# Two experts of a routed feed-forward layer: whole-array matmuls in three passes on weights split in high and low parts

## The chip, the cores and the metric

One core of one Trainium2 chip runs the whole program. The metric is the device time of one execution, in microseconds (us); lower is better. In the kernel's names, PE is TensorE, DVE is VectorE, ACT is ScalarE and SP is SyncE, whose queue issues the DMAs.

## The reference

Two trunk layers work on 256 latent tokens and 256 context tokens of width 1024: a gMLP mixer and a dense SwiGLU, then a bidirectional recurrent mixer and a layer of eight SwiGLU experts of which each latent token uses two. Only the expert layer is touched. With `h` of 256 x 1024 and expert width 3584:

```
logits = h @ w_router                                  # 256 x 8
top_val, top_idx = top_k(logits, 2);  probs = softmax(top_val)
combine[t, e] = probs of expert e for token t, or 0
for e in range(8):
    out += combine[:, e:e+1] * ((silu(h @ w_gate[e]) * (h @ w_up[e])) @ w_down[e])
```

All arrays are float32. An expert works only on the tokens routed to it; each expert's three weight matrices are 44 MB, and all eight are read from memory once.

## The kernel before

**Ranks and units.** Expert 0 is rank 0 whatever its load, because its weights are fetched before the routing is known. The other seven are ranked by their number of tokens, rank 1 the fullest; SP reads the ranked order from registers, so the addresses of the weights are chosen on the chip (`wsrc`, line 406). A one-hot matmul gathers the tokens of an expert into up to 128 columns (`gather`, line 1230). `units` (line 1173) decides from the counts how a rank runs: with up to 32 tokens its matmuls use 32 columns of the array, four of them side by side (n = 4); with up to 64 they use 64, two side by side (n = 2); with more they use all 128 (n = 1). Ranks 0 to 3 can have an overflow unit for tokens beyond the base unit: a count of 65 to 96 gives a base of 64 and the rest as overflow, a count above 128 a base of 128 and the rest as overflow. The choice is a branch on registers: `tc.If` in `region` (line 1339). Rank 1 takes n = 2 or n = 1, ranks 2 and 3 one of all three.

**Chunks.** The expert width is cut in seven chunks of 512. A chunk needs six slots of weights of 1 MB each (128 x 2048): two of gate, two of down, two of up. `chunk` (line 1289) does them in that order: transposes of the hidden values of an earlier chunk, the gate projection (`proj`, line 1272, matmuls on line 1276), the down projection of the earlier chunk (line 1303), the up projection. Gate and up are 8 matmuls of 512 columns each, down is 8 too. The trace has two records for each float32 matmul. For n > 1 `total` (line 1279) adds the side-by-side partial sums on ACT and DVE. After the base unit the overflow unit, if there is one, runs the same six slots again (`over`, line 1319, tile `xu`).

**Two lanes.** `moe_regions` (line 161) writes the order out by hand. One lane is the ranks 1, 2, 3, the other 0, 7, 6, 5, 4; their chunks are interleaved in proportion to their bytes. `R` is a chunk, `F` a last down projection, `O` and `G` the gathers, `S` the weighted scatter at an expert's end. The down projection lags its gate and up by one chunk in the first lane, two in the second. Two chunks of ranks 1 or 2 never follow each other directly.

**Slots.** `Stream` (line 192) owns a ring of SBUF slots of 1 MB. In the expert stage there are 16: four of `rawp`, one of `raw2`, six of `hlp`, two of `hl2` and three of `raw3` (`RAW3`, line 158). SP issues the loads in the order in which the regions use them; a load waits until its slot has been read by its last reader. For ranks 0 to 3 that is the overflow unit or, without one, the end of the branch on line 1364.

**Three passes.** The dense layers already split their operands. `prep_to` (line 239) casts a weight slot to `float32r` on ACT (`wh`) and subtracts on DVE (`wl`); `mm3` (line 505) then does three matmuls instead of one float32 matmul: high x high, high x low, low x high. A `float32r` matmul is one record.

Of the kernel before, what the change touches and what calls it, by code (L numbers as in the profile page):

```python
# [9 lines left out]
F32 = mybir.dt.float32  # L10
F32R = mybir.dt.float32r
# [143 lines left out]

TM = (1, 1, 1, 0)
WC = (2, 2, 14)
RAW3 = ("wx", "wy", "wz")


def moe_regions():
# [25 lines left out]


LAG = {r: 1 if r in (1, 2, 3) else 2 for r in range(NE)}


class Stream:
# [34 lines left out]
        self.slots += slots  # L227
        self.load()

    def take_raw(self, n):  # L230
        got = [self.raw.pop(self.prep_i + k) for k in range(n)]
        self.prep_i += n
        return got

    def free(self, got):
        self.slots += [s for s, _ in got]
# [32 lines left out]
def block_kernel(ctx, tc, xin, pos, cst, rows, wsT, adaS, adaT, wA, lruG, wr, wM, out):  # L269
# [136 lines left out]
    def wsrc(r, k):  # L406
        if r == 0:
            return wM[k]
        return lambda: wM[bass.ds(base42[r] + k, 1)].rearrange("o p c -> (o p) c")

    for kind, r, c in regs:
        if kind in "RF":
            for w in ("g", "d", "u"):
                cc = c - LAG[r] if w == "d" else c
                if 0 <= cc < NCH:
                    items += [(wsrc(r, 6 * cc + 2 * "gud".index(w) + i), "own") for i in range(2)]
    st = Stream(nc, items, 2)
    st.add_h(hlp, 3)
    st.nh = 0

# [84 lines left out]
    def mm3(o, lh, ll, rh, rl, start, stop):  # L505
        PE.matmul(o, lh, rh, start=start, stop=False)  # L506
        PE.matmul(o, lh, rl, start=False, stop=False)  # L507
        PE.matmul(o, ll, rh, start=False, stop=stop)  # L508
# [620 lines left out]
        ACT.preload_act_table_set("sqrt_and_others")  # L1129
    c_y(0)  # L1130
    c_y(1)
    st.moe([(hlp, f"w{x}{i}") for i in range(3) for x in "hl"] + [(hl2, "wh0"), (hl2, "wl0")])
    hx = hTp.tile([P, 4, D], F32, tag="hTlo", name="hx")
    h2, hg, tg = hx[:, 0:2], hx[:, 2].rearrange("p (n c) -> p n c", n=2), hx[:, 3].rearrange("p (n c) -> p n c", n=2)
    lb = [bank(), bank()]
# [37 lines left out]
    def units(q):  # L1173
        few, m64, cb_, co_ = q[:, 6:10], q[:, 10], q[:, 11], q[:, 12]
        cf = q[:, 4]
        DVE.tensor_scalar(m64, cf, 64.0, 64.0, op0=ALU.is_gt, op1=ALU.mult)
        DVE.scalar_tensor_tensor(m64, cf, 96.0, m64, op0=ALU.is_le, op1=ALU.mult)
        if q is Qr:
            DVE.memset(m64[:, 4:NE], 0.0)
        DVE.tensor_scalar(co_, cf, -128.0, None, op0=ALU.add)  # L1180
        DVE.tensor_add(co_, co_, m64)
        DVE.tensor_scalar(co_, co_, 0.0, None, op0=ALU.max)
        DVE.tensor_sub(cb_, cf, co_)
        for n, (v, lim, m) in enumerate(((cb_, 64, 64), (cb_, 32, 32), (co_, 32, 64), (co_, 32, 32))):
            DVE.tensor_scalar(few[:, n], v, float(lim), -float(m), op0=ALU.is_le, op1=ALU.mult)

    units(Q)
    dup = mp.tile([P, 2, P], F32, name="dup")
# [41 lines left out]
    def gather(x, G, k0, b):  # L1230
        for kk in range(4):
            for t in range(2):
                PE.matmul(b[:, kk * P:(kk + 1) * P], h2[:, t, (k0 + kk) * P:(k0 + kk + 1) * P], G[:, t], start=(t == 0), stop=(t == 1))  # L1233
        xq = x[:, k0:k0 + 4].rearrange("p k s -> p (k s)")
        if k0:
            DVE.tensor_copy(xq, b)
        else:
            ACT.copy(xq, b)

    def gather_parts(E):  # L1240
        G = m2.tile([P, 2, P], F32, tag=f"G{E.s}", bufs=1, name="G")
        sl_ = m2.tile([P, P], F32, tag="sl", bufs=1, name="sl")
        x = m2.tile([P, 8, P], F32, tag=f"x{E.s}", bufs=1, name="x")
        GT = m2.tile([P, 256], F32, tag=f"GT{E.s}", name="GT")
        ps = m2.tile([P, 1], F32, tag=f"ps{E.s}", name="ps")
        E.base = Unit(x, None, tg[:, E.s], GT, ps)

        def last():
            weigh(E, G, GT, ps, nb[0]())
            E.rv = nc.values_load(cnti[0:1, 0, E.e:E.e + 1], engines=ENG, min_val=0, max_val=128)  # L1250
            if E.e < 4:
                E.ro = nc.values_load(cnti[0:1, 1, E.e:E.e + 1], engines=ENG, min_val=0, max_val=128)
            if E.e in (1, 2, 3):
                E.rl = nc.values_load(cnti[0:1, 3, E.e:E.e + 1], engines=ENG, min_val=0, max_val=1)
        return [lambda: onehot(E, G, sl_, 0), lambda: gather(x, G, 0, nb[0]()), lambda: gather(x, G, 4, nb[0]()), last]

# [32 lines left out]
    def chunk(U, n, bt, bg, bu, yb_, raws, first, last, hd, hw, hook=None):  # L1289
        rg, rd, ru = raws  # L1290
        m = P // n
        if rd:
            for kk in range(4):
                PE.transpose(bt[:, kk * m:(kk + 1) * m], hd[0:m, kk * P:(kk + 1) * P], ident[0:m, 0:m])  # L1294
            ACT.copy(U.th[:, 0:4 * m], bt[:, 0:4 * m])  # L1295
        if rg:
            proj(bg, U.x, rg, n)
            ACT.activation(hw[0:m], total(bg, n), AF.Silu)
        if rd:
            for kk in range(4):  # L1300
                r, g = divmod(kk, n)
                for hf in range(2):
                    PE.matmul(yb_[hf][m * g:m * g + m], U.th[:, kk * m:(kk + 1) * m], rd[hf][1][:, kk * 512:(kk + 1) * 512],  # L1303
                              start=(first and r == 0), stop=(last and r == 4 // n - 1), **tp(n, g))
        if rd and hook is not None:
            hook()
        if ru:
            proj(bu, U.x, ru, n)
            DVE.tensor_mul(hw[0:m], hw[0:m], total(bu, n))  # L1309

    def scatter(GT, src):
# [27 lines left out]
    def region(E, c, raws):  # L1339
        p0, p1 = bks[2 * par[0]:2 * par[0] + 2]  # L1340
        lag = LAG[E.e]
        a = (p1, p0, p1, E.base.y, raws, c == lag, c == NCH + lag - 1, *hsel(E, c, E.hh))

        def few_():
            if E.e == 1:
                return chunk(E.base, 2, *a)
# [5 lines left out]
        if E.e in (1, 2, 3):  # L1352
# [61 lines left out]
    pp = ctx.enter_context(tc.tile_pool(name="pp", bufs=1, space=bass.MemoryType.PSUM))  # L1414
    *bks, y0, y1, y2, y3 = [pp.tile([P, 512], F32, tag=f"b{i}", name="ps") for i in range(8)]
    Ys = [mw.tile([P, D], F32, name=f"Y{n}") for n in range(2)]
    Gu = mw.tile([P, 2, P], F32, name="Gu")
    slu = mw.tile([P, P], F32, name="slu")
    ta_ = mw.tile([P, 512], F32, name="ta_")
# [20 lines left out]
    def yrot(E):  # L1440
# [2 lines left out]
            return E.base.y[cyc[0] % 2]  # L1443
        return f
    parts = {}
    for kind, e, c in regs:
        if kind == "O":
            exps[e] = Expert(e, Qr)
            parts[e] = gather_parts(exps[e])
            parts[e][0]()  # L1450
        elif kind == "G":
            for f in parts[e][1:]:
                f()
            start(exps[e])
        elif kind == "S":
            E = exps[e]
            nb[0] = yrot(E)
            scatter(E.base.GT, Ys[E.s])
            if e < 4:
                with tc.If(E.ro > 0):  # L1460
                    DVE.tensor_scalar(E.over.y, E.over.y, E.over.ps, None, op0=ALU.mult)  # L1461
                    scatter(E.over.GT, E.over.y)
            nb[0] = rot
        else:
            E = exps[e]
            par[0] ^= 1
            rg = st.take_raw(2) if c < NCH else None
            rd = st.take_raw(2) if c >= LAG[e] else None
            ru = st.take_raw(2) if c < NCH else None
            region(E, c, (rg, rd, ru))  # L1470
# [44 lines left out]
```

## Time and profile before

| | us |
|---|---|
| three runs | 1848.4, 1852.88, 1853.86 |
| median | 1852.88 |
| the profiled execution | 1844.61 |
| its span | 1842.8 |

The profile is of one further execution, 1.8 us longer than its span and 8.3 us below the median of the runs. The expert stage begins at about 850 us and ends at about 1830 us of the span. A name such as L1276 is a line of the code; a tile such as `raw` is a weight slot. In a table of windows the number after a time is a count of instructions, PEclk is the granted TensorE clock as a share of full speed, and the DMA share is that of the 16 DMA engines together.

### The profile page before, as it was taken

How to read it: one execution, taken by the hardware profiler on the slowest of the kernel's cores; microseconds unless marked ns; L12 is line 12 of the kernel's file. 1: busy time of each engine (PE TensorE's matmuls, PEld its weight loads, DVE VectorE, ACT ScalarE, POOL GpSimd, SP SyncE). 2: the span in 40 equal slices, each digit the busy share in tenths (PEclk: the TensorE clock that was granted, in tenths of full speed). 3: DMA queues.
4: the chain of work that ended last, by engine and by line, in shares of the span. 5: the costliest groups of instructions: out<-in, count | busy, mean ns of one | idle time of the engine just before them, and what ended most of it. 6: DMA issues, size and time to landing. Idle time of an engine off the chain costs nothing. (4 is left out here: it accounts for less than half of the span.)

```text
span 1842.8 us, 21730 instructions
## 1 busy us (share of the span) xinstructions
PE 1667.9 (91%) x8192; PEld 1026.5 (56%) x8192; DVE 835.5 (45%) x1342; ACT 573.8 (31%) x840; POOL 19.4 (1%) x22
## 2 busy tenths in 40 slices
PE   5999999999999999985878789989987999889987
PEld 2888888988888888764434233343333353333332
DVE  3777745569875348985322222333110112132234
ACT  5624224732222247972221121211120112122221
POOL 0000001000000000001000000000000000000000
PEclk9999999999999999997989999999998999999999
DMA  8554424247765313265896778987899899979990
GB/s 362 207 182 160 160 92 155 92 160 254 262 260 206 116 67 115 92 256 234 324 415 281 319 301 340 404 358 295 363 418 418 365 395 360 387 323 387 401 389 24
DMA packets 70421, 492.97 MB, mean 268 GB/s; under 512 B 7968, under 2 KB 8160, under 8 KB 11872
## 3 DMA queue, kind: packets, MB, share of 16 engines
q1 hardware_dynamic: 70240, 490.45, 67.5%
q8 instruction: 127, 2.08, 0.5%
q14 instruction: 54, 0.44, 0.1%
HBM read 489.34 MB, written 1.08 MB: 266 GB/s over the span
## 5 line engine op out<-in xcount | busy, mean ns | idle before, releaser
L1276 PE MATMUL ps<-raw,x 128*64 128x512 f32 (+2 forms) x1792 | 439.9, 610 | 28.0 <-issue 24.9
L1276 PEld LDWEIGHTS ps<-raw,x 128*64 128x64 f32 (+2 forms) x1792 | 163.1, 143 | 260.2 <-issue 247.4
L1303 PE MATMUL ps<-raw,hx 128*32 128x512 f32 (+2 forms) x1120 | 256.5, 616 | 19.3 <-ACT hx L1295 15.1
L522 PE MATMUL ps<-hThi,wh 128*128 128x512 f32 (+1 forms) x736 | 254.4, 347 | 3.0 <-ACT hThi L373 3.0
L523 PE MATMUL ps<-hTlo,wh 128*128 128x512 f32 (+1 forms) x736 | 251.7, 343 | 1.4 <-DVE hTlo L374 1.3
L524 PE MATMUL ps<-hThi,wl 128*128 128x512 f32 (+1 forms) x736 | 252.4, 343 | 0.0
L1283 DVE TENSOR_TENSOR ta__6629<-ps,ta__6629 64x512 f32<-64x512 f32 x112 | 76.5, 683 | 348.8 <-ACT ta__6629 L1282 348.8
L249 ACT CAST wh<-raw 128x2048 fp32r<-128x2048 f32 x69 | 131.6, 1910 | 227.5 <-PE ps L523 114.1
L250 DVE TENSOR_TENSOR wl<-raw,wh 128x2048 fp32r<-128x2048 f32 x69 | 158.8, 2304 | 63.7 <-ACT wh L249 63.0
L1303 PEld LDWEIGHTS ps<-raw,hx 128*32 128x32 f32 (+2 forms) x1120 | 92.1, 137 | 160.5 <-issue 125.2
L388 DVE SCALAR_TENSOR_TENSOR dj<-raw,srow 128x1024 bf16<-128x1024 f32 x128 | 156.2, 1220 | 36.2 <-DMA raw<-in_adaT_dram 32.6
L1282 ACT COPY ta__6629<-ps 64x512 f32<-64x512 f32 x112 | 65.2, 582 | 301.1 <-PE ps L1276 291.1
L522 PEld LDWEIGHTS ps<-hThi,wh 128*128 128x128 f32 x736 | 138.0, 188 | 21.3 <-ACT hThi L373 3.7
L523 PEld LDWEIGHTS ps<-hTlo,wh 128*128 128x128 f32 x736 | 138.1, 188 | 20.8 <-DVE hTlo L374 2.0
L524 PEld LDWEIGHTS ps<-hThi,wl 128*128 128x128 f32 x736 | 138.1, 188 | 18.3 <-issue 0.5
L1309 DVE TENSOR_TENSOR hx<-hx,ps 128x512 f32<-128x512 f32 x14 | 9.6, 688 | 254.9 <-PE ps L1276 179.3
L506 PE MATMUL ps<-wh,ph 128*128 128x512 f32 x304 | 119.4, 393 | 0.0
L508 PE MATMUL ps<-wh,pl 128*128 128x512 f32 x304 | 118.5, 390 | 0.6 <-DVE pl L753 0.5
L507 PE MATMUL ps<-wl,ph 128*128 128x512 f32 x304 | 118.3, 389 | 0.0
L1295 ACT COPY hx<-ps 128x128 f32<-128x128 f32 (+2 forms) x70 | 25.3, 362 | 224.6 <-PE ps L1294 222.8
L1276 PE MATMUL ps<-raw,xu 128*32 128x512 f32 x448 | 69.7, 635 | 21.7 <-DVE accy L1331 11.5
L1286 DVE TENSOR_TENSOR ta__6629<-ps,ta__6629 32x512 f32<-32x512 f32 x70 | 47.5, 678 | 38.0 <-ACT ps L1285 34.2
(327 smaller groups left out, 1672.5 us busy)
## 6 DMA issues: line engine op xcount, KB each, us to landing
raw<-in_wM_dram SPq DMA_DIRECT2D x336, 1024.0 KB, 13.6
raw<-in_wA_dram SPq DMA_DIRECT2D x69, 1024.0 KB, 4.9
raw<-in_adaT_dram SPq DMA_DIRECT2D x40, 1024.0 KB, 4.9
va<-in_adaS_dram SPq DMA_DIRECT2D x4, 1024.0 KB, 11.2
ysum<-in_xin_dram SPq DMA_DIRECT2D x4, 512.0 KB, 5.5
vb<-in_adaS_dram SPq DMA_DIRECT2D x2, 1024.0 KB, 11.9
srow<-in_adaS_dram SPq DMA_DIRECT2D x2, 1024.0 KB, 13.2
lw<-in_lruG_dram SPq DMA_DIRECT2D x8, 256.0 KB, 3.3
```

Source lines behind the costliest of these rows:

```text
L249: self.nc.scalar.copy(wh, raw)
L250: self.nc.vector.tensor_tensor(out=wl, in0=raw, in1=wh.bitcast(F32), op=ALU.subtract)
L388: DVE.scalar_tensor_tensor(j, raw[:, kk * D:(kk + 1) * D], 1.0, srow[:, vv], op0=ALU.mult, op1=ALU.mult, accum_out=adaC[l, bb // 8][:, bb ...
L506: PE.matmul(o, lh, rh, start=start, stop=False)
L507: PE.matmul(o, lh, rl, start=False, stop=False)
L508: PE.matmul(o, ll, rh, start=False, stop=stop)
L522: PE.matmul(o, wh[:, r], hThi[:, kk, c0:c1], start=(kk == 0), stop=False)
L523: PE.matmul(o, wh[:, r], hTlo[:, kk, c0:c1], start=False, stop=False)
L524: PE.matmul(o, wl[:, r], hThi[:, kk, c0:c1], start=False, stop=(kk == 7))
L1276: PE.matmul(o[m * g:m * g + m], x[:, kb, 0:m], raws[kb // 4][1][:, (kb % 4) * 512:(kb % 4 + 1) * 512], start=(r == 0), stop=(r == 8 // n - ...
L1283: DVE.tensor_tensor(out=ta_[0:64], in0=o[0:64], in1=ta_[0:64], op=ALU.add)
L1303: PE.matmul(yb_[hf][m * g:m * g + m], U.th[:, kk * m:(kk + 1) * m], rd[hf][1][:, kk * 512:(kk + 1) * 512], start=(first and r == 0), stop= ...
```

## The change

Ranks 1 and 2 lose their branches. Their base unit always takes up to 128 tokens, and every matmul with a weight is done by `mm3` in `float32r`. The gathered tokens are split in `xh` and `xl`, the transposed hidden values in the two tiles `thl`. The weights are split in pieces of a quarter slot (128 x 512): a cast on ACT, a subtraction on DVE. The split pieces live in a ring of four pairs (`wp`); piece n + 4 is made after the three matmuls of piece n are issued, and four pieces of a chunk's first slot are made ahead, before the region that comes before the chunk. In the order of the loads that first slot moves ahead of the up slots of that earlier region. The ring takes the place of two raw slots (`hl2`), and one slot of `raw3` is dropped, so that 13 of 16 slots are left. Rank 3 and the second lane run as before, and so does the overflow of ranks 1 and 2 beyond 128 tokens.

```
-RAW3 = ("wx", "wy", "wz")
+RAW3 = ("wx", "wy")
+THREE = (1, 2)
...
+def moe_slots(regs):
+    runs = [o for o in regs if o[0] in "RF"]
+    lists = [region_slots(o) for o in runs]
+    for a, b, x, y in zip(runs, runs[1:], lists, lists[1:]):
+        if a[1] not in THREE and b[1] in THREE:
+            n = sum(k[2] != "u" for k in x)
+            x.insert(n, y.pop(0))
+    return [k for x in lists for k in x]
...
-    st.moe([(hlp, f"w{x}{i}") for i in range(3) for x in "hl"] + [(hl2, "wh0"), (hl2, "wl0")])
+    st.moe([(hlp, f"w{x}{i}") for i in range(3) for x in "hl"])
+    wp = [hl2.tile([P, 4, 512], F32R, tag=f"w{x}0", name=f"w{x}p") for x in "hl"]
...
         if q is Qr:
+            DVE.memset(m64[:, 1:3], 0.0)
             DVE.memset(m64[:, 4:NE], 0.0)
...
+        if q is Qr:
+            DVE.memset(few[:, 0:2, 1:3], 0.0)
...
+        if isinstance(x, tuple):
+            xh, xl_ = [z[:, k0:k0 + 4].rearrange("p k s -> p (k s)") for z in x]
+            ACT.copy(xh, b)
+            DVE.tensor_tensor(out=xl_, in0=b, in1=xh.bitcast(F32), op=ALU.subtract)
+            return
...
+    def piece(key, kk, n):
+        raw = st.peek(key)[:, kk * 512:(kk + 1) * 512]
+        wh, wl = wp[0][:, n % 4], wp[1][:, n % 4]
+        ACT.copy(wh, raw)
+        DVE.tensor_tensor(out=wl, in0=raw, in1=wh.bitcast(F32), op=ALU.subtract)
+        return wh, wl
...
+    def whole(E, op, bt, bg, bu):
+        c = op[2]
+        hw = hsel(E, c, E.hh)[1]
+        prep(op, 4)
+        ps = pieces(op)
+        xh, xl_ = E.base.x
+        yb_ = E.base.y
+        if any(k[2] == "d" for k, _ in ps):
+            for kk in range(4):
+                PE.transpose(bt[:, kk * P:(kk + 1) * P], hw[:, kk * P:(kk + 1) * P], ident)
+            ACT.copy(thl[0], bt)
+            DVE.tensor_tensor(out=thl[1], in0=bt, in1=thl[0].bitcast(F32), op=ALU.subtract)
+        for n, ((_, _, w, i), kk) in enumerate(ps):
+            wh, wl = ahead[op][n]
+            kb = 4 * i + kk
+            if w == "d":
+                q = slice(kk * P, (kk + 1) * P)
+                mm3(yb_[i], thl[0][:, q], thl[1][:, q], wh, wl, c == 1 and kk == 0, c == NCH and kk == 3)
+            else:
+                mm3(bg if w == "g" else bu, xh[:, kb], xl_[:, kb], wh, wl, kb == 0, kb == 7)
+            prep(op, n + 5)
+            if w == "g" and kb == 7:
+                ACT.activation(hw, bg, AF.Silu)
+            if w == "u" and kb == 7:
+                DVE.tensor_mul(hw, hw, bu)
...
-        if E.e in (1, 2, 3):
+        if E.e in THREE:
+            whole(E, op, p1, p0, p1)
+        elif E.e == 3:
             with tc.If(E.rl > 0) as c1:
...
+            if n + 1 < len(runs) and e not in THREE and runs[n + 1][1] in THREE:
+                prep(runs[n + 1], 4)
```

## Rows read from the trace of the kernel before

**Rows 1.** The page: engines; a group of the dense layers (busy us, mean ns)
```profile
PE 1667.9 (91%) x8192; PEld 1026.5 (56%) x8192; DVE 835.5 (45%) x1342; ACT 573.8 (31%) x840; POOL 19.4 (1%) x22
...
L522 PE MATMUL ps<-hThi,wh 128*128 128x512 f32 (+1 forms) x736 | 254.4, 347 | 3.0 <-ACT hThi L373 3.0
```

**Rows 2.** Table of windows, by stages of the first lane: ranks 1, 2 and 3
```profile
core 0: us, PE busy (x) PEld busy (x) DVE busy (x) ACT busy (x) POOL busy (x), PEclk, DMA share, GB/s
903.00:1228.00 325.00, 276.45 (x1313) 114.89 (x1314) 78.39 (x120) 66.68 (x123) 0.00 (x0) 0.96 0.87 355
1228.00:1513.00 285.00, 257.73 (x1049) 110.51 (x1049) 56.14 (x94) 41.60 (x77) 0.00 (x0) 0.98 0.90 367
1513.00:1821.00 308.00, 277.62 (x1438) 109.70 (x1436) 78.86 (x118) 66.03 (x123) 0.00 (x0) 0.97 0.85 346
```

**Rows 3.** Waits over 903 to 1513: who waited for whom, total, times, longest (us)
```profile
SPq L222 <- PE ps L1276: 166.8, 50, 26.9
SPq L222 <- PEq L1364: 123.2, 11, 20.0
SPq L222 <- PE ps L1303: 55.2, 14, 18.8
PEld ps L1276 <- DMA raw<-in_wM_dram: 9.2, 16, 2.3
```

**Rows 4.** Groups by shape over 903 to 1513: busy us, mean ns | idle before
```profile
L1276 PE MATMUL ps<-raw,x 128*128 128x512 f32 x448 | 199.0, 598 | 1.5 <-issue 0.7 <-PEq L1364 0.7
L1303 PE MATMUL ps<-raw,hx 128*128 128x512 f32 x223 | 100.9, 606 | 1.5 <-ACT hx L1295 0.8 <-ACTq L1261 0.7
L1276 PE MATMUL ps<-raw,xu 128*32 128x512 f32 x224 | 32.8, 596 | 7.9 <-DVE accy L1331 5.8 <-DVE accy L1329 1.2 <-DVE hx L1309 1.0
```

**Rows 5.** Timeline of PE, a full-array chunk of rank 1: start, duration (us)
```profile
1091.89 0.66 PE L1294 MATMUL ps<-ident,hx 128*128 128x128 f32 x4
1092.38 7.03 PE L1276 MATMUL ps<-raw,x 128*128 128x512 f32 x16
1099.25 7.03 PE L1303 MATMUL ps<-raw,hx 128*128 128x512 f32 x16
1106.12 7.03 PE L1276 MATMUL ps<-raw,x 128*128 128x512 f32 x16
```

**Rows 6.** Table of windows, a stretch of the dense layers in three passes
```profile
450.00:500.00 50.00, 50.00 (x220) 41.12 (x219) 45.98 (x71) 12.29 (x10) 0.00 (x0) 1.00 0.74 265
```

**Rows 7.** Timeline of ACT and DVE in the dense layers: splits of 512 columns
```profile
369.63 1.28 DVE L612 TENSOR_TENSOR pl<-gu,ph 128x512 fp32r<-128x512 f32 x2
378.17 1.13 ACT L611 CAST ph<-gu 128x512 fp32r<-128x512 f32 x2
503.22 0.62 ACT L611 CAST ph<-gu 128x512 fp32r<-128x512 f32 x1 [4.05 <-DVE gu L802]
503.88 0.69 DVE L612 TENSOR_TENSOR pl<-gu,ph 128x512 fp32r<-128x512 f32 x1 [0.69 <-ACT ph L611]
```

**Rows 8.** Timeline of a chunk of the second lane that comes before a chunk of rank 1
```profile
1121.90 0.43 PE L1294 MATMUL ps<-ident,hx 32*128 32x32 f32 x4
1122.26 1.92 PE L1276 MATMUL ps<-raw,x 128*32 128x512 f32 x16
1124.01 0.27 ACT L1295 COPY hx<-ps 128x128 f32<-128x128 f32 x1
1124.33 1.09 PE L1303 MATMUL ps<-raw,hx 128*32 128x512 f32 x8 [0.15 <-ACT hx L1295]
```

**Rows 9.** Table of windows, two stretches in the stages of ranks 1 and 2
```profile
1171.00:1203.00 32.00, 27.62 (x104) 11.28 (x102) 6.18 (x10) 6.18 (x11) 0.00 (x0) 1.00 1.01 419
1313.00:1432.00 119.00, 101.98 (x403) 43.63 (x402) 16.24 (x26) 16.79 (x31) 0.00 (x0) 0.94 1.01 418
```

**Rows 10.** Timeline of PE over 1313 to 1432: down projections of rank 2
```profile
1321.26 7.03 PE L1303 MATMUL ps<-raw,hx 128*128 128x512 f32 x16
...
1401.34 7.03 PE L1303 MATMUL ps<-raw,hx 128*128 128x512 f32 x16
```

More of the change, by code (lines that the diff above doesn't have):

```diff
@@ L189, with region_slots @@
 LAG = {r: 1 if r in (1, 2, 3) else 2 for r in range(NE)}
+def region_slots(op):
+    kind, r, c = op
+    out = []
+    for w in "gdu":
+        cc = c - LAG[r] if w == "d" else c
+        if 0 <= cc < NCH:
+            out += [(r, cc, w, i) for i in range(2)]
+    return out
+def moe_slots(regs):
[6 more added lines that the diff above has]
+    return [k for x in lists for k in x]
 class Stream:
@@ L228, in moe, with take_raw, peek @@
         self.load()
[L230 to L233, printed above, removed]
+    def take_raw(self, keys):
+        return [self.raw.pop(self.pos[k]) for k in keys]
+    def peek(self, key):
+        return self.raw[self.pos[key]][1]
     def free(self, got):
@@ L409, in wsrc @@
         return lambda: wM[bass.ds(base42[r] + k, 1)].rearrange("o p c -> (o p) c")
[L411 to L416, printed above, removed]
+    mpos = {}
+    for key in moe_slots(regs):
+        r, cc, w, i = key
+        mpos[key] = len(items)
+        items.append((wsrc(r, 6 * cc + 2 * "gud".index(w) + i), "own"))
     st = Stream(nc, items, 2)
+    st.pos = mpos
     st.add_h(hlp, 3)
@@ L1242, in gather_parts @@
         sl_ = m2.tile([P, P], F32, tag="sl", bufs=1, name="sl")
-        x = m2.tile([P, 8, P], F32, tag=f"x{E.s}", bufs=1, name="x")
+        if E.e in THREE:
+            x = (m2.tile([P, 8, P], F32R, tag=f"x{E.s}", bufs=1, name="xh"), m2.tile([P, 8, P], F32R, tag="xl", bufs=1, name="xl_"))
+        else:
+            x = m2.tile([P, 8, P], F32, tag=f"x{E.s}", bufs=1, name="x")
         GT = m2.tile([P, 256], F32, tag=f"GT{E.s}", name="GT")
@@ L1249, in last @@
             weigh(E, G, GT, ps, nb[0]())
-            E.rv = nc.values_load(cnti[0:1, 0, E.e:E.e + 1], engines=ENG, min_val=0, max_val=128)
+            if E.e not in THREE:
+                E.rv = nc.values_load(cnti[0:1, 0, E.e:E.e + 1], engines=ENG, min_val=0, max_val=128)
             if E.e < 4:
                 E.ro = nc.values_load(cnti[0:1, 1, E.e:E.e + 1], engines=ENG, min_val=0, max_val=128)
-            if E.e in (1, 2, 3):
+            if E.e == 3:
                 E.rl = nc.values_load(cnti[0:1, 3, E.e:E.e + 1], engines=ENG, min_val=0, max_val=1)
@@ L1309, in chunk, with pieces, prep @@
             DVE.tensor_mul(hw[0:m], hw[0:m], total(bu, n))
+    ahead = {}
+    def piece(key, kk, n):
[4 more added lines that the diff above has]
+        return wh, wl
+    cnt = [0]
+    def pieces(op):
+        return [(k, kk) for k in region_slots(op) for kk in range(4)]
+    def prep(op, n):
+        got = ahead.setdefault(op, [])
+        ps = pieces(op)
+        while len(got) < min(n, len(ps)):
+            got.append(piece(*ps[len(got)], cnt[0]))
+            cnt[0] += 1
+    def whole(E, op, bt, bg, bu):
+        c = op[2]
+        hw = hsel(E, c, E.hh)[1]
+        prep(op, 4)
+        ps = pieces(op)
+        xh, xl_ = E.base.x
[11 more added lines that the diff above has]
+                mm3(yb_[i], thl[0][:, q], thl[1][:, q], wh, wl, c == 1 and kk == 0, c == NCH and kk == 3)
+            else:
+                mm3(bg if w == "g" else bu, xh[:, kb], xl_[:, kb], wh, wl, kb == 0, kb == 7)
[4 more added lines that the diff above has]
+                DVE.tensor_mul(hw, hw, bu)
     def scatter(GT, src):
@@ L1337, in hsel, with region @@
         return hh[(c - lag) % lag], hh[c % lag]
-    def region(E, c, raws):
+    def region(E, op, raws):
+        c = op[2]
         p0, p1 = bks[2 * par[0]:2 * par[0] + 2]
@@ L1344, in few_ @@
         def few_():
-            if E.e == 1:
-                return chunk(E.base, 2, *a)
             with tc.If(E.rv > 32) as c2:
@@ L1350, in few_ @@
                 chunk(E.base, 4, *a)
-        if E.e in (1, 2, 3):
+        if E.e in THREE:
+            whole(E, op, p1, p0, p1)
+        elif E.e == 3:
             with tc.If(E.rl > 0) as c1:
@@ L1416, in block_kernel @@
     Ys = [mw.tile([P, D], F32, name=f"Y{n}") for n in range(2)]
+    thl = [mw.tile([P, 512], F32R, name=f"th{x}") for x in "hl"]
     Gu = mw.tile([P, 2, P], F32, name="Gu")
@@ L1445, in block_kernel @@
     parts = {}
+    runs = [o for o in regs if o[0] in "RF"]
     for kind, e, c in regs:
@@ L1466, in block_kernel @@
             par[0] ^= 1
[L1467 to L1470, printed above, removed]
+            op = (kind, e, c)
+            n = runs.index(op)
+            if n + 1 < len(runs) and e not in THREE and runs[n + 1][1] in THREE:
+                prep(runs[n + 1], 4)
+            keys = region_slots(op)
+            rg, rd, ru = [[(None, st.peek(k)) for k in keys if k[2] == w] or None for w in "gdu"]
+            region(E, op, (rg, rd, ru))
+            rg, rd, ru = [st.take_raw([k for k in keys if k[2] == w]) for w in "gdu"]
             for r in (rg, rd, ru):
```

## Prediction

> **What bounds the kernel now.** First the busy times of the whole span: PE is busy 91%, DVE 45%, ACT 31% [rows 1]. That is an average over two kinds of work, so next the expert stage by windows. They follow the first lane: rank 1 (903 to 1228), rank 2 (1228 to 1513), rank 3 (1513 to 1821). PE is busy 85%, 90% and 90% of them, and at the same time the DMA engines are busy 87%, 90% and 85% [rows 2]. Two resources are near their end, so a saving on one meets the other. The waits say which ends last today: PE waits for a weight slot for about 9 us in 610, while SP waits for PE to give slots back 167 + 123 + 55 = 345 us [rows 3]. PE is the bound, and the DMA idles because the 16 slots are full. There are stretches where it does not idle: 1171 to 1203 and 1313 to 1432 run at a DMA share of 1.01 and 418 GB/s [rows 9]. One slot (1.049 MB) costs 1.049/418 = 2.51 us there.
>
> **Which experts are touched.** Two experts have 7 x 24 = 336 matmuls, 672 float32 records. On the full array there are 448 + 223 [rows 4] (one is missing from the trace), all between 903 and 1513, so ranks 1 and 2 already run n = 1 on these inputs, 14 chunks. The change replaces full-array float32 by full-array passes; it doesn't widen anything. The 32-column overflow in the same windows (tile `xu`) is rank 1's and stays.
>
> **The change part by part.**
>
> *Matmuls.* 8 float32 matmuls of 512 columns go from 1099.25 to 1106.12, 6.87 us [rows 5], 0.859 us each. The dense layers put 220 `float32r` matmuls of the same shape, with the same 128-column weight loads, into 50.00 us [rows 6]: 0.2273 us each, 0.682 us for three. A chunk falls from 24 x 0.859 = 20.6 to 16.4 us. Over 336 matmuls PE gets back 336 x 0.177 = **59 us**. Transposes stay (0.66 us a chunk [rows 5]).
>
> The Trainium skill (TensorE: Matmul & The Clock Gate, "Wait — 56ns, not 53.3ns?") gives warm matmuls of 512 columns 215.7 ns start to start. By it the passes would cost 0.647 us and PE would get back 71 us. The trace shows 227.3 ns for exactly this pattern, so the trace's number stands.
>
> *Splitting.* Each chunk adds 24 casts on ACT and 24 subtractions on DVE of 128 x 512. Back to back they step by less than their durations: two subtractions take 1.28 us, so the second starts 1.28 - 0.69 = 0.59 us (call it 0.60) after the first; two casts step by 1.13 - 0.62 = 0.51 us [rows 7]. DVE then has 24 x 0.60, one subtraction of the hidden values and the gate product: 26 x 0.60 = 15.6 us in a chunk in which PE works 0.7 + 16.4 = 17.1 us. ACT has about 26 x 0.51 = 13.3. Both fit, DVE with 9% to spare.
>
> The ring must also cover the latency. The last matmul of piece n starts 0.45 us into its triple and ends 0.35 us later (the mean of such a matmul [rows 1]). A hand-over is 0.04 us (503.22 + 0.62 to 503.88 [rows 7]), taken as 0.05 at each of three steps. Then cast 0.62 and subtraction 0.69: the low part of piece n + 4 is ready at 0.45 + 0.35 + 0.62 + 0.69 + 0.15 = 2.26 us. It is wanted at 4 x 0.682 + 0.227 = 2.95 us. So PE stays the pace inside a chunk, with 0.7 us in hand. I charge 0.2 us for each of 16 regions (14 chunks and two last down projections) for the start: 3 us.
>
> *Pieces made ahead.* Four casts and four subtractions stand in the queues of ACT and DVE before the region that precedes each of the 16. What is queued behind them there is the copy of the transposed hidden values (L1295), for which PE's down projection waits. Today that copy comes just in time: it ends at 1124.28 and PE has lost 0.15 us [rows 8]. Four casts are 4 x 0.51 = 2.0 us. If ACT and DVE do them while the overflow unit before them still runs, they cost nothing; if they stand where the program has them, 2.0 us each time. From 0 to 33 us over 16; I take the middle, **16 us**, because the rows show both kinds of neighbour (an idle ACT in rank 2's stage, a chain of copies in rank 1's).
>
> *Branches.* Ranks 1 and 2 lose one or two branches a region. The nearest row is a PE wait for its own queue at L1364, 0.7 us in the stage [rows 4]; gain between 0 and 16 x 0.7 = 11 us, taken as 0, since the branch for the overflow stays.
>
> *DMA.* The bytes are the same. In the stretch at 1.01 nothing can end earlier than the loads. Three chunks of rank 2 lie in 1313 to 1432 [rows 10] (the first and the last of the three stand there); their saving of 4.2 - 1.1 us each is lost: **9 us**. The shorter ring has three slots less landed when such a stretch begins: 3 x 2.51 = **7.5 us**, charged once. From 0 (PE still sets the pace, as for 9 us in 610 now) to once in each of the 14 chunks; once is nearest to the waits for slots that the rows show. Rank 3's stage has a DMA share of 0.85 and no change on PE: from 0 to 7.5 us more, taken as 0.
>
> *Small things.* The split of the gathered tokens, the zeroed flags and the split of the hidden values (hidden behind the 5.5 us of the gate's passes) are taken as nothing; uncovered they would be about 1.4 us for each of two gathers.
>
> Sum: -59 + 3 + 16 + 9 + 7.5 = **-24 us**. Against the profiled execution, 1844.6 us (span 1842.8), that is 1821 us; the median of the runs lies 8.3 us above it, so **1829 us**.
>
> **The rivals.**
>
> 1. *The whole PE saving arrives.* The pieces ahead are hidden and the queue has always a slot ready. For it: PE waited for slots only 9 us [rows 3]. Against: with 59 us less, the stage of rank 2 would need a DMA share of 0.90 x 285/(285 - 29.5) = 1.00 throughout [rows 2]. Time: 1852.9 - 59 + 3 = 1797 us.
> 2. *ACT and DVE are the pace.* If a piece costs 0.76 us instead of 0.682 (a blocked queue, a subtraction that waits), 336 x 0.08 = 27 us come on top: 1856 us. At 0.859 nothing is gained inside the chunks. Against: 0.60 a piece in rows 7.
>    The Trainium skill (VectorE: DVE Perf Modes, "The DRAIN you can't avoid") has a rule that speaks for it: the next VectorE operation does not start until the pipe of the one before is empty. By it a subtraction steps by its whole 0.69 us, DVE needs 26 x 0.69 = 17.9 us a chunk against PE's 17.1, and 14 x 0.8 = 11 us are added: 1840 us. Here the trace disagrees, 0.59 us from start to start [rows 7], so this form has 3 in 100 within this rival.
> 3. *The ring of 13 slots runs dry in every chunk: slower.* A chunk of rank 1 holds its six slots to the end of its overflow, about 29 us today (1092 to 1121, rows 5 and 8). Ten other slots are 10 x 2.51 = 25 us of loads; seven are 17.6. If the 7.5 us are paid in each of 14 chunks, not once, the sum is -24 + 13 x 7.5 = +74 us: 1927 us. It decides from the fourth payment on: -24 + 3 x 7.5 is zero. For it: SP's single waits reach 27 us [rows 3]. Against: a DMA engine that idles in a chunk has no debt, and the chunk itself gets 4 us shorter.
> 4. *The change does not do what it says* (the experts were not on the full array before, so three passes would be more work): excluded by rows 4.
>
> **How the numbers follow.** The forecast's case (a gain of 8 to 45 us) has 0.55, rival 1 0.12, rival 2 0.16, rival 3 0.13, small mixtures 0.04. The predicted time is the forecast's, 1829 us. The range goes from rival 1 with a little of the branches, 1795, to rival 2, 1856, which leaves out rival 3 and the mixtures. About 0.3% (5.6 us) is what a measurement of this kernel can tell from no change. Faster by more: 0.55 + 0.12 and 0.05 of rival 2 = 0.72. Within: 0.12. Slower: 0.13 and 0.03 of rival 2 = 0.16.
>
> **What would show it.** In the new profile 72 matmuls of a chunk at 0.227 us start to start, 16.4 us; PE waits for ACT or DVE within a chunk near zero (else rival 2); the casts of the pieces ahead directly before the chunk before, and the wait of the down projection there near 1 us; a DMA share of 0.92 to 1.0 over ranks 1 and 2; PE's waits for weight slots up from 9 to about 25 us (more than 60: rival 3); rank 3's stage of 308 us unchanged. The prediction is wrong if another order of the instructions lets PE work elsewhere while it waits, or if the pieces wait for one another.

## The result, and the profile after

The changed kernel takes **1919.6 us** (median of 4 runs, 1917.78 to 1923.15) against 1851.28 us for the kernel before (4 runs beside it): a ratio of 1.0372, 95% interval 1.0348 to 1.0396. It is 3.7% slower. The forecast was 1829 us, with a range up to 1856; the prediction was wrong in sign and in size.

The page of the changed kernel first (the engines; three groups with busy us, mean ns | idle before; its span is 1916.0 us):

```profile
PE 1666.2 (87%) x8528; PEld 1116.8 (58%) x8528; DVE 1064.3 (56%) x1696; ACT 769.6 (40%) x1178; POOL 19.4 (1%) x22
...
L1351 ACT CAST whp<-raw 128x512 fp32r<-128x512 f32 x336 | 197.3, 619 | 50.8 <-PE ps L530 35.9
...
L528 PE MATMUL ps<-whp,xh 128*128 128x512 f32 x224 | 106.0, 473 | 52.8 <-ACT whp L1351 47.4
...
L529 PE MATMUL ps<-wlp,xh 128*128 128x512 f32 x224 | 106.3, 475 | 14.0 <-DVE wlp L1352 13.7
```

PE is busy as long as before, 1666 against 1668 us [rows 1]: on this view the three passes have saved nothing. And PE idles ahead of the passes, for pieces that ACT has still to cast. The table of windows of the changed kernel, over the stretches of rows 2 and the 95 us from there to the end of its span, says where:

```profile
903.00:1228.00 325.00, 252.41 (x1348) 145.78 (x1349) 175.54 (x269) 151.07 (x265) 0.00 (x0) 0.87 0.79 321
1228.00:1513.00 285.00, 222.90 (x1137) 133.84 (x1136) 152.72 (x242) 126.22 (x226) 0.00 (x0) 0.92 0.82 333
1513.00:1821.00 308.00, 271.24 (x1354) 122.51 (x1354) 94.33 (x147) 77.23 (x141) 0.00 (x0) 0.97 0.89 357
1821.00:1916.00 95.00, 75.49 (x373) 27.56 (x369) 33.30 (x53) 20.54 (x41) 4.25 (x3) 0.95 0.60 242
```

Three columns fall together in the first two stretches: PE's busy time by 24 and 35 us, the granted clock from 0.96 and 0.98 to 0.87 and 0.92, and the DMA share from 0.87 and 0.90 to 0.79 and 0.82 [rows 2]. The forecast had expected DMA shares of 0.92 to 1.0. So the loads are not what holds it up; something keeps PE waiting and cold. The whole loss lies in the stages of ranks 1 and 2: PE's last whole-array matmul with a weight ends at 1513.9 us in the kernel before and at 1587.4 us here, and from there to PE's last matmul it takes 319 us in both. The waits of PE from 850 us on (total, times, longest):

```profile
PE ps L528 <- ACT whp L1351: 51.7, 23, 4.3
PE ps L529 <- DVE wlp L1352: 16.9, 21, 1.4
...
PE ps L1376 <- DVE hx L1344: 8.3, 2, 4.7
...
PE ps L1376 <- DVE hb L1344: 7.2, 2, 3.6
```

L1376 are the transposes at the start of a whole-array chunk, L528 and L529 the first two passes of each piece. In the kernel before, PE idled 1.5 + 1.5 us ahead of its whole-array matmuls with weights in all [rows 4]. The timeline of PE over one such chunk, of rank 1, shows how they come about (start, duration; in brackets PE's idle time and who ended it):

```profile
1090.13 5.88 PE L1311 MATMUL ps<-raw,x 128*32 128x512 f32 x32 [0.91 <-PEq L1545]
1100.68 1.09 PE L1376 MATMUL ps<-ident,hx 128*128 128x128 f32 x4 [4.68 <-DVE hx L1344]
1103.09 0.80 PE L528 MATMUL ps<-whp,xh 128*128 128x512 f32 x1 [1.32 <-ACT whp L1351]
...
1104.41 0.63 PE L530 MATMUL ps<-whp,xl__6798 128*128 128x512 f32 x1
...
1108.25 0.44 PE L530 MATMUL ps<-whp,xl__6798 128*128 128x512 f32 x1
1108.62 0.43 PE L1329 MATMUL ps<-ident,hb 32*128 32x32 f32 x4
1108.99 1.92 PE L1311 MATMUL ps<-raw,x 128*32 128x512 f32 x16
1110.73 1.94 PE L1338 MATMUL ps<-raw,hx 128*32 128x512 f32 x16
1112.44 1.94 PE L1311 MATMUL ps<-raw,x 128*32 128x512 f32 x16
1117.09 0.50 PE L528 MATMUL ps<-whp,xh 128*128 128x512 f32 x1 [2.70 <-ACT whp L1351]
1118.47 0.72 PE L529 MATMUL ps<-wlp,xh 128*128 128x512 f32 x1 [0.89 <-DVE wlp L1352]
```

Read it from the top. A chunk of the second lane ends (L1311, `x`, 32 columns). Then come the four transposes and twelve passes, four pieces, of the rank 1 chunk. Then **another whole chunk of the second lane** (L1329 to L1311, 1108.62 to 1114.38). Only then the other 60 passes. In the source the rank 1 chunk stands behind that second chunk as a whole. Its start has been moved ahead. Counted over the trace, 15 of the 16 regions of ranks 1 and 2 (14 chunks and two last down projections) are torn in this way, 13 of them after the twelfth pass.

The move costs time at three places. The transposes stand too early: they wait 4.68 us. They write the same PSUM bank as the up projection of the chunk before, and so wait until ACT and DVE have added its four partial sums and multiplied them (L1344). The passes that follow are slow: from 1104.41 to 1108.25 nine of them step by 0.427 us instead of 0.23. And behind the chunk of the second lane PE waits again, 2.70 + 0.89 us, because pieces five to eight are cast only after that chunk's sums. ACT in the same kernel shows this last point:

```profile
1115.81 0.58 ACT L1320 COPY ps<-ta__6629 32x512 f32<-32x512 f32 x1 [0.75 <-DVE ta__6629 L1318]
1116.41 2.18 ACT L1351 CAST whp<-raw 128x512 fp32r<-128x512 f32 x4
```

The slow steps are the clock. Windows over this chunk of the changed kernel (the last three columns are the granted clock, the DMA share and GB/s):

```profile
1100.60:1104.40 3.80, 2.40 (x6) 1.50 (x7) 1.98 (x4) 2.57 (x5) 0.00 (x0) 0.50 1.04 435
1104.40:1108.20 3.80, 3.80 (x10) 2.97 (x9) 1.16 (x2) 0.20 (x1) 0.00 (x0) 0.50 0.22 91
...
1117.00:1122.00 5.00, 4.02 (x10) 2.94 (x11) 4.29 (x8) 2.83 (x6) 0.00 (x0) 0.66 1.00 415
1122.50:1127.80 5.30, 5.30 (x24) 4.30 (x23) 4.51 (x8) 4.96 (x10) 0.00 (x0) 1.00 0.94 394
```

Behind the wait of 4.68 us the clock is at 0.50, its lower level of 1.2 GHz, although the passes now follow one another without a gap. Behind the second wait it is 0.66 on the mean of 5 us, and only then 1.00.

**Where PE's time went.** The table adds up PE's time from 850 us of each profiled execution to its last matmul. Each matmul counts from its start to the start of the next, or to the end of the work issued so far if that comes first; what is left is idle. The small transposes with 32 or 64 columns (22 to 23 us in every column) and the 10 us behind the last matmul are left out. The sums of the columns differ from that of the column "before" by what the spans differ by, within 2 us.

| us | before | after | e1 | e5 | e9 |
|---|---|---|---|---|---|
| matmuls with whole-array weights (672 float32 records before, 1008 passes in the others) | 295.9 | 291.6 | 248.9 | 248.7 | 280.7 |
| matmuls with 32 columns of the array | 215.5 | 218.5 | 230.7 | 224.3 | 213.7 |
| matmuls with 64 columns (rank 3 and two ranks of the second lane) | 226.2 | 222.2 | 223.6 | 223.4 | 223.7 |
| other 128-column matmuls (gathers, scatters, transposes) | 93.5 | 98.7 | 99.1 | 98.9 | 99.7 |
| idle | 127.3 | 201.9 | 156.5 | 151.0 | 189.8 |
| span | 1842.8 | 1916.0 | 1842.3 | 1829.8 | 1891.1 |

From before to after: 75 us more idle time and only 4 us less for the passes, where 59 had been forecast. e1, e5 and e9 are experiments below.

### The profile page after: what moved, and what is told of

Its sections match the earlier page's. It is cut to its first block, busy times and chain, and to the rows that moved or that the text cites. A ratio compares the mean times of both kernels' runs of the same rounds, so it can differ in the third digit from the quotient of the medians.

```text
span 1916.0 us, 23350 instructions
## 1 busy us (share of the span) xinstructions
PE 1666.2 (87%) x8528; PEld 1116.8 (58%) x8528; DVE 1064.3 (56%) x1696; ACT 769.6 (40%) x1178; POOL 19.4 (1%) x22
## 5 line engine op out<-in xcount | busy, mean ns | idle before, releaser
L1311 PE MATMUL ps<-raw,x 128*32 128x512 f32 (+1 forms) x1344 | 243.8, 617 | 17.7 <-DVE sl L1252 8.4
L1352 DVE TENSOR_TENSOR wlp<-raw,whp 128x512 fp32r<-128x512 f32 x336 | 219.4, 686 | 34.1 <-ACT whp L1351 32.0
L1351 ACT CAST whp<-raw 128x512 fp32r<-128x512 f32 x336 | 197.3, 619 | 50.8 <-PE ps L530 35.9
L1338 PE MATMUL ps<-raw,hx 128*32 128x512 f32 (+1 forms) x896 | 156.0, 610 | 14.0 <-ACT hx L1330 12.1
L1311 PEld LDWEIGHTS ps<-raw,x 128*32 128x32 f32 (+1 forms) x1344 | 78.0, 126 | 145.4 <-issue 140.9
L528 PE MATMUL ps<-whp,xh 128*128 128x512 f32 x224 | 106.0, 473 | 52.8 <-ACT whp L1351 47.4
L528 PE MATMUL ps<-wh,ph 128*128 128x512 f32 x304 | 119.4, 393 | 0.0
L529 PE MATMUL ps<-wlp,xh 128*128 128x512 f32 x224 | 106.3, 475 | 14.0 <-DVE wlp L1352 13.7
L529 PE MATMUL ps<-wl,ph 128*128 128x512 f32 x304 | 118.3, 389 | 0.0
L1338 PEld LDWEIGHTS ps<-raw,hx 128*32 128x32 f32 (+1 forms) x896 | 49.7, 121 | 98.2 <-issue 75.5
## 6 DMA issues: line engine op xcount, KB each, us to landing
raw<-in_wM_dram SPq DMA_DIRECT2D x336, 1024.0 KB, 11.4
```

Of the source, the lines that this page charges most:

```text
L1311: PE.matmul(o[m * g:m * g + m], x[:, kb, 0:m], raws[kb // 4][1][:, (kb % 4) * 512:(kb % 4 + 1) * 512], start=(r == 0), stop=(r == 8 // n - ...
L1351: ACT.copy(wh, raw)
L1352: DVE.tensor_tensor(out=wl, in0=raw, in1=wh.bitcast(F32), op=ALU.subtract)
```

## The experiments

**The theories.** *Order*: a branch with its body keeps its place as one block in each engine's order, while plain instructions outside a branch are placed one by one when the kernel is built. By taking ranks 1 and 2 out of their branches, the change let their first transposes and passes slip ahead of the chunk before. *Slots* (rival 3 of the prediction): the ring with 13 slots runs dry in every chunk. *Pace* (rival 2): ACT and DVE can't make pieces fast enough.

### e1: the chunk kept as one block

```
-            if E.e not in THREE:
-                E.rv = nc.values_load(...)
+            E.rv = nc.values_load(...)
...
         if E.e in THREE:
-            whole(E, op, p1, p0, p1)
+            with tc.If(E.rv > 0):
+                whole(E, op, p1, p0, p1)
```

> The changed kernel with the three-pass chunks of ranks 1 and 2 put in a branch that is always taken on these inputs, so that the chunk stays one block in the order of PE. Order theory (the loss comes from the four first pieces of a chunk being issued ahead of the region before it, with PE waits of 3 to 5 us on both sides of that region and the clock at 1.2 GHz after them): the 83 us of additional PE idle time and the clock go, 1810 to 1845 us, granted clock of ranks 1 and 2 back at 0.96 or more. Slots theory (the ring of 13 runs dry in each chunk): still 1890 us or more, since the slots are the same. Pace theory (ACT and DVE set the pace of the pieces): 1870 us or more.

Measured: **1840.26 us**, ratio to before 0.9949 (0.9929 to 0.997). A branch that is always taken gives back 79 us of 1919.6 (78 by the ratios; the experiments did not all run on one chip, but each had the kernel before beside it). None of the 16 regions is torn in its trace. The windows of e1:

```profile
903.00:1228.00 325.00, 264.25 (x1532) 149.78 (x1524) 193.69 (x300) 166.56 (x295) 0.00 (x0) 0.93 0.89 362
1228.00:1513.00 285.00, 242.62 (x1221) 145.98 (x1220) 168.99 (x267) 140.63 (x247) 0.00 (x0) 0.95 0.90 369
...
1100.50:1110.00 9.50, 9.50 (x42) 7.74 (x42) 9.19 (x15) 8.31 (x14) 0.00 (x0) 1.00 1.01 419
```

The DMA share is back at that of rows 2 and the clock most of the way (0.93 and 0.95, where 0.96 or more was expected). The last row is a stretch inside a rank 1 chunk: 42 passes in 9.50 us, 0.226 us each, with PE never idle, at a DMA share of 1.01, while ACT and DVE are busy 8.3 and 9.2 us of the 9.5. That ends *pace*: PE sets it inside a chunk, as forecast, though DVE has 3% to spare there where 9% had been forecast. The passes take 248.9 us in all (table), 47 less than the float32 matmuls. What is left to find: idle time is still 29 us above before.

### e2: the kernel before with 13 slots

```
-RAW3 = ("wx", "wy", "wz")
+RAW3 = ("wx", "wy")
...
-    st.moe([(hlp, f"w{x}{i}") for i in range(3) for x in "hl"] + [(hl2, "wh0"), (hl2, "wl0")])
+    st.moe([(hlp, f"w{x}{i}") for i in range(3) for x in "hl"])
```

> The kernel before with 13 raw slots instead of 16 and nothing else changed. Slots theory: 1900 us or more, the loss of the changed kernel without its passes. Order theory: 0 to 10 us more than before, 1850 to 1862 us, because PE, not the loads, ends last there.

Measured: 1849.7 us, ratio 1.0002 (0.9987 to 1.0016). Three slots fewer cost this kernel nothing, and the three-pass kernel with the same 13 slots takes 1840 us when its chunks are blocks (e1). Rival 3 falls, though its time of 1927 us was the nearest to the result.

### e3: the kernel before with ranks 1 and 2 out of their branch

```
-        if E.e in (1, 2, 3):
+        if E.e in (1, 2):
+            chunk(E.base, 1, *a)
+        elif E.e == 3:
             with tc.If(E.rl > 0) as c1:
```

> The kernel before with the branch of ranks 1 and 2 taken away alone: the full-array float32 chunks stand as plain instructions, without pieces. Order theory: only the transposes and a few instructions of a chunk move ahead of the region before it; a part of the loss, 5 to 30 us more than before (the transposes wait for the chain of sums of the region that used their bank). If the loss needs the pieces, within 3 us of before. A gain of up to 11 us if the branches themselves cost.

Measured: 1860.26 us, ratio 1.006 (1.0043 to 1.0076). The same float32 matmuls, without the branch, are 0.6% slower. PE in this kernel, at the place of the timeline above:

```profile
1086.28 3.64 PE L1276 MATMUL ps<-raw,x 128*32 128x512 f32 x32 [0.76 <-PEq L1462]
1095.11 0.89 PE L1294 MATMUL ps<-ident,hx 128*128 128x128 f32 x4 [5.20 <-DVE hx L1309]
1095.93 0.63 PE L1294 MATMUL ps<-ident,hb 32*128 32x32 f32 x4
```

and the first window of the same kernel:

```profile
903.00:1228.00 325.00, 271.94 (x1235) 107.23 (x1231) 73.98 (x113) 62.38 (x115) 0.00 (x0) 0.92 0.81 327
```

The four transposes of rank 1 have slipped ahead of the second lane's chunk (`hb`, 32 x 32) and wait 5.20 us; in the kernel before that wait is absent [rows 5]. The clock of the stretch falls from 0.96 to 0.92, the DMA share from 0.87 to 0.81 [rows 2]. So the slip needs no passes and no pieces, but with float32 matmuls it is mainly the transposes that slip, and it costs 10 us instead of 79. Counted as in the table above, idle time in e3 is only 3 us more than in the kernel before; its matmuls with 32 columns take 10 us more and the other 128-column matmuls, the transposes among them, 7 us more. What the slip costs here shows as a lower clock rather than as waiting.

### e4: one block, no pieces made ahead

```
-            if n + 1 < len(runs) and e not in THREE and runs[n + 1][1] in THREE:
-                prep(runs[n + 1], 4)
```

(on e1)

> As the first of this call, without the four pieces made ahead of the region before a chunk: each chunk starts with cast and subtraction of its first piece in the open, about 1.4 us plus the queue of the region before. Order theory: 16 regions times 1.5 to 4 us more than with the pieces ahead, 25 to 60 us. If the pieces ahead cost as much in the region before (2 us each) as they save, within 10 us.

Measured: 1870.2 us, ratio 1.0114 (1.0092 to 1.0136), 30 us above e1. PE then waits for the first pieces (waits of PE of e4 from 850 us on):

```profile
PE ps L528 <- ACT whp L1350: 25.5, 12, 4.3
...
PE ps L1337 <- ACT hx L1329: 12.2, 17, 3.4
```

So the pieces made ahead are worth 30 us. But they have a price, visible in the second row: the wait of the down projection for its copy is 12.2 us here and 33.5 in e1.

### e5 and e6: the pieces ahead, later

In e1 the four casts stand ahead of the whole chunk before. ACT and PE of e1 at such a place:

```profile
1086.47 2.18 ACT L1350 CAST whp<-raw 128x512 fp32r<-128x512 f32 x4
1088.67 0.27 ACT L1329 COPY hx<-ps 128x128 f32<-128x128 f32 x1
...
1088.99 3.67 PE L1337 MATMUL ps<-raw,hx 128*32 128x512 f32 x16 [5.50 <-ACT hx L1329]
```

The copy of 0.27 us stands behind 2.18 us of casts, and PE waits 5.50 us for it. In the kernel before it waits 3.48 us at this place (down projection at 1086.69), without any casts, for the sums of the chunk before. e5 writes the four pieces into the branches of that chunk, behind its down projection; e6 directly behind the copy.

```
-            if n + 1 < len(runs) and e not in THREE and runs[n + 1][1] in THREE:
-                prep(runs[n + 1], 4)
+            pre = runs[n + 1] if n + 1 < len(runs) and e not in THREE and runs[n + 1][1] in THREE else None
...
# chunk(), e5:
         if rd and hook is not None:
             hook()
+        if pre is not None:
+            prep(pre, 4)
         if ru:
# chunk(), e6: the same two lines behind ACT.copy(U.th...)
```

> The changed kernel with its whole-array chunks kept in a branch (as in e1_unit), and the four pieces made ahead issued behind the down projection of the region before, not ahead of that region. Queue theory (the casts of the pieces stand on ScalarE, partly waiting for their loads, ahead of the copy that the down projection of the region before needs; in e1_unit TensorE waited 33.5 us in 21 waits at that place, against 11.6 us in the kernel before): these waits fall back to about 12 us and the time falls by 15 to 25 us against e1_unit, to about 1815 to 1825. Work theory (the eight instructions have to stand somewhere on ScalarE and VectorE, and behind the down projection they delay the sums of the up projection and the first passes as much): within 5 us of e1_unit, 1835 to 1845, with the waits moved to the first passes and to the sums.

> As e5_unit_pieces_behind_down, with the four pieces issued right behind the copy of the transposed activations, ahead of the gate's sums. Queue theory: the down projection no longer waits, but the gate's sums and its SiLU stand behind four casts (4 x 0.66 us and any wait for a load), which matter only if the up projection or the next region waits for them: 1815 to 1830. Work theory: within 5 us of e1_unit, 1835 to 1845.

Measured: e5 **1830.45 us**, ratio 0.9893 (0.9869 to 0.9917); e6 1831.81 us, ratio 0.9895 (0.9872 to 0.9918). Both are some 10 us below e1, less than the 15 to 25 that the queue theory had expected and more than the work theory's 5. The wait in question, in e1, in e5, and the timeline of ACT in e5 at the place that was shown for e1:

```profile
PE ps L1337 <- ACT hx L1329: 33.5, 21, 5.5
```

```profile
PE ps L1337 <- ACT hx L1329: 26.0, 19, 4.3
```

```profile
1087.07 0.62 ACT L1352 CAST whp<-raw 128x512 fp32r<-128x512 f32 x1
1087.71 0.27 ACT L1329 COPY hx<-ps 128x128 f32<-128x128 f32 x1
1087.87 1.66 ACT L1352 CAST whp<-raw 128x512 fp32r<-128x512 f32 x3
```

It fell by 7.5 us, not by the 21 of the queue theory. The ACT rows of e5 show one reason: inside the branch, too, the order is not that of the source, and one of the four casts still stands ahead of the copy. At this place most of the wait (4.11 us) is that of the sums of the chunk before, which ACT has ahead of it. At three other places the cast itself waits for the load of its weight slot, and the copy and PE wait behind it. One of them, on ACT and on PE:

```profile
1308.29 0.62 ACT L1352 CAST whp<-raw 128x512 fp32r<-128x512 f32 x1 [3.82 <-DMA raw<-in_wM_dram]
...
1309.24 2.62 PE L1337 MATMUL ps<-raw,hx 128*32 128x512 f32 x12 [4.30 <-ACT hx L1329]
```

PE loses 2.19, 4.30 and 3.65 us there, 10.1 of the 26.0; in e1 three such places make 11.4 of the 33.5 us. The intervals of e1 and e5 don't overlap (0.9929 and up, up to 0.9917), so the gain is one, and e5 is faster than both kernels of this case: 1.07% or 19.8 us below the kernel before.

### e7: one pass

The two low passes and the subtractions are left out of e5, and the casts go to ACT and DVE in turn; the output lacks the low parts.

```
-                mm3(bg if w == "g" else bu, xh[:, kb], xl_[:, kb], wh, wl, kb == 0, kb == 7)
+                PE.matmul(bg if w == "g" else bu, xh[:, kb], wh, start=(kb == 0), stop=(kb == 7))
```

(and the same for the down projection)

> As e5_unit_pieces_behind_down, with the two low passes of the whole-array chunks left out, and the subtractions that make the low parts of the weights with them (the casts are dealt out to ScalarE and VectorE in turn); the output lacks the low parts. 672 passes of 0.2273 us less, 153 us of TensorE. Load theory (the loads of the 918 us between 903 and 1821 already fill 0.87 to 0.90 of the DMA engines, so no more than about 100 us can be had there): the time falls by 60 to 100 us to 1730 to 1780, the DMA share of the three stretches rises to 0.95 or more and TensorE waits for raw weights. TensorE theory (the passes set the pace and the loads give way): it falls by more than 120 us, below 1710. Neither (waits between the engines set it): it falls by less than 40 us with the DMA share at 0.90.

Measured: 1774.0 us, ratio 0.9593 (0.9567 to 0.9619): 75 us below before and 56 below e5 (60 to 100 were expected), for 153 us less of passes at the warm pace. The windows of e7:

```profile
903.00:1228.00 325.00, 237.01 (x1342) 99.89 (x1334) 137.02 (x252) 128.31 (x232) 0.00 (x0) 0.88 0.96 394
1228.00:1513.00 285.00, 221.63 (x1035) 99.52 (x1034) 89.89 (x172) 92.42 (x166) 0.00 (x0) 0.85 1.01 416
```

Here are the DMA shares of 0.96 and 1.01 that the forecast had looked for; ranks 1 and 2 end at 1442 us in e7, so the second window holds some 70 us of rank 3's stage, and the third stretch, in which the program ends, has 0.68. The load theory holds for ranks 1 and 2: the casts wait for loads for 55 us on DVE and 42 on ACT, and the gain is far below 153 us. As e7 does strictly less work than e5, its 75 us below the kernel before are a fair bound for what three passes could win in this order of the work.

### e8: two blocks, an attempt at the order

7 chunks of e1 were written as two blocks, transposes and four pieces ahead of the chunk before, the rest behind it.

```
+                    with tc.If(exps[o2[1]].rv > 0):
+                        whole(exps[o2[1]], o2, q1, q0, q1, 0, 4)
             region(E, op, (rg, rd, ru))
```

> The changed kernel with its whole-array chunks kept in branches (as in e1_unit), but 7 of the chunks written in two blocks: the transposes and the twelve passes of the first four pieces in a block of their own ahead of the region before, and the other passes behind that region, which is the order that TensorE had in the changed kernel. Nothing else differs from e1_unit. Order theory (the order alone costs the 79 us between the changed kernel and e1_unit, about 5.3 us for each of some 15 chunks): 7 x 5.3 = 37 us more than e1_unit, 1868 to 1885, with a wait of 3 to 5 us ahead of the transposes and slow passes behind it in each of the seven. Branch theory (the branch helped in e1_unit by something else, such as when loads are issued or what other engines do between blocks): 1832 to 1850.

Measured: 1858.41 us, ratio 1.0037 (1.0024 to 1.005), 18 us above e1; between the two expectations, and it did not try what it was meant to. In its trace the early block stands behind the chunk before after all:

```profile
1127.12 1.92 PE L1310 MATMUL ps<-raw,x 128*32 128x512 f32 x16
1128.97 0.66 PE L1376 MATMUL ps<-ident,hx 128*128 128x128 f32 x4
1132.49 0.80 PE L528 MATMUL ps<-whp,xh 128*128 128x512 f32 x1 [2.86 <-ACT whp L1350]
```

Blocks are moved too, then, but as wholes: none of the 16 regions is torn. The first pieces had moved along, so 7 chunks ran as in e4, with pieces made late: 7/15 of e4's 30 us is 14, and 18 were measured. On the order it says nothing.

### e9: the order of the changed kernel, by hand

Ten chunks of e1: the transposes and the passes of the first four pieces as plain instructions, the region before bound behind the last of them, the other passes in a branch.

```
+                whole(exps[o2[1]], o2, q1, q0, q1, 0, 4)
+                with tc.issue_after(lastz[0].ins):
+                    region(E, op, (rg, rd, ru))
```

> The changed kernel with its whole-array chunks kept in branches (as in e1_unit), but for 10 of them the transposes, the first four pieces and their twelve passes are plain instructions ahead of the region before, and that region is bound by hand behind the last of the twelve passes; the other 60 passes stay in a branch behind it. (In e8_split_blocks the build had set the early blocks behind the region before after all, so that kernel tried only four late pieces in 7 chunks.) Order theory (this order costs the 79 us between the changed kernel and e1_unit, some 5.3 us for each of about 15 chunks): 53 us more than e1_unit, 1880 to 1905, with waits of 3 to 5 us ahead of the transposes, slow passes behind them and a second wait behind the region in each of the ten. Branch theory (the branch helped by something else than the order): 1835 to 1860.

Measured: **1897.63 us**, ratio 1.0249 (1.0219 to 1.0278): 57 us more than e1 (56 by the ratios) for ten chunks, 53 expected. Its timeline of PE, and then a window of it with the clock:

```profile
1095.97 1.09 PE L1375 MATMUL ps<-ident,hx 128*128 128x128 f32 x4 [6.86 <-DVE hx L1343]
1098.42 0.79 PE L528 MATMUL ps<-whp,xh 128*128 128x512 f32 x1 [1.36 <-ACT whp L1350]
...
1104.70 1.92 PE L1310 MATMUL ps<-raw,x 128*32 128x512 f32 x16
...
1113.61 0.50 PE L528 MATMUL ps<-whp,xh 128*128 128x512 f32 x1 [2.70 <-ACT whp L1350]
1115.00 0.80 PE L529 MATMUL ps<-wlp,xh 128*128 128x512 f32 x1 [0.89 <-DVE wlp L1351]
```

```profile
1099.00:1103.00 4.00, 4.00 (x10) 3.08 (x10) 1.90 (x4) 0.93 (x2) 0.00 (x0) 0.50 0.99 410
```

All the signs of the changed kernel are back: the wait ahead of the transposes, the clock of 0.50 behind it, and the second wait of 2.70 + 0.89 us behind the chunk of the second lane. In the table, e9 has 33 us more idle time than e1 and 32 us more in the same 1008 passes. The instructions are those of e1; what differs is their order, on ACT and DVE as on PE (pieces five to eight are cast behind the region), and that the first twelve passes stand outside the branch. Exactly ten regions are torn in its trace. The order is the cause: 5.7 us for each chunk that is torn in two, against 79/15 = 5.3 us in the changed kernel.

## Why the prediction was wrong, point by point

- **The bound.** That PE sets the end, not the loads, was right; e1's DMA shares stayed at those of before. PE's own waits for weights did not rise to 25 us. In the whole-array chunks ACT reads the weight slots now, and its casts wait for loads: 4.9 us in the changed kernel, 20.3 in e1, 26.8 in e5.
- **Matmuls, -59 us.** The pace was right: 0.226 us a pass inside a chunk (e1), against 0.2273 [rows 6]. The Trainium skill's 215.7 ns (TensorE: Matmul & The Clock Gate, "Wait — 56ns, not 53.3ns?") is not reached here either. But the sum multiplied that warm pace by all 1008 passes. They took 291.6 us in the changed kernel, a gain of 4, and 248.9 in e1, a gain of 47: 20 us above 1008 x 0.2273 even there. Of these 20, 14 lie in 74 passes that step by more than 0.33 us; in the changed kernel there are 252 such passes, with 57 us.
- **Splitting, +3 us.** ACT and DVE keep up (e1's window). The start of a chunk was charged 0.2 us; e1 has 7.9 us in 9 waits for the low part of a chunk's early piece, 0.88 each time.
- **Pieces made ahead, +16 us.** Near: in e1 the down projection's wait is 33.5 us against 15.1 in the kernel before over the same part of the trace, 18 us more. Moving the pieces (e5) gave 10 us back. Without the pieces ahead the time is 30 us longer (e4). What the prediction did not have is that a cast made ahead can wait for its load and hold up the copy behind it (11.4 of the 33.5 us).
- **Branches, 0 us.** This is the step that failed. The prediction asked what a branch costs and found a gain between 0 and 11 us. It did not ask what the branch does to the order: it takes for granted that a chunk runs as it is written, from its transposes to its last pass. The changed kernel gave that up, and it cost 79 us (from e1), with the opposite sign. The last sentence of the prediction names another order of the instructions as what would upset it, but as something that would help PE.
- **DMA, +9 us.** Not measured by itself; the casts that wait for loads, above, are the part of it that the traces show. e7 shows that the limit is real, and that it lies some 75 us below the kernel before.
- **Fewer slots, +7.5 us.** Nothing in the float32 kernel (e2); for the three-pass kernel no run separates it.
- **Rank 3's stage unchanged.** Right: from the last whole-array matmul to PE's last it is 318.9 us before and 318.5 after.
- **The rivals.** 1: excluded by the result. 2: false, by e1's window: 0.226 us a pass, and 9.19/15 = 0.61 us for an instruction of DVE, not 0.69. 3: its 1927 us came within 8 us of the result with a mechanism that e2 excludes; a time that fits is no evidence for a cause. 4: excluded, as said; e1 shows the three passes doing less work than the float32 matmuls.

With the chunk as one block the sum of -24 us would have been measured as -9.4 us (e1, from the ratio's 0.51%), and with the pieces moved as -19.8 (e5). That e5 stands at 1830 where 1829 was forecast is partly an accident: its passes save 47, not 59, its idle time grows by 24, and the matmuls with 32 columns by 9.

The 43 us that the passes of the changed kernel take longer than those of e1 fall on both sides of the tear: the first twelve passes of the 16 regions take 69.8 us against 50.1, the other 816 take 221.8 against 198.8.

What stays open: no run separates the early transposes from the late pieces five to eight, and none shows how much of the 26.0 us that PE still waits in e5 for the copy could be had by loads that come earlier.

## What to carry to other kernels

In this kernel a branch around a piece of work is also what keeps other work from being set between its instructions; if an edit takes work out of a branch, or puts it into one, look at the order of the instructions on each engine around it before costing anything else. A start that is made early pays only if nothing stands between it and the rest: here it waited for the sums of the chunk before, ran cold, and held up the next chunk. Work made ahead in a queue that also serves the present chunk must have its data there: a cast that waits for its load holds up the copy behind it. And count a saving on TensorE at the clock that the stretch really has, not at the warm pace.

## What the hardware showed that was not expected

- A wait of 4.68 us was followed by passes at a granted clock of 0.50 for at least 3.8 us without a gap between them (window 1104.40 to 1108.20): the wait is paid for a second time. Over the 1008 passes this is 43 us between the changed kernel and e1, as much as the added idle time (45 us).
- Taking away three of the sixteen weight slots of 1 MB did not change the time of the kernel before (e2: 1.0002), although SP waits for slots for 345 us of 610 [rows 3]: a long wait of the loads for slots does not show that more slots would help.
